# Eight mLSTM heads woven into projection products: 18 steps a head in place of 16, and the norm's products kept in VectorE's program order

## The chip, the cores and the metric

One Trainium2 chip, of which the kernel uses one core. The metric is the device time of one execution in microseconds (us). A core has a matrix engine (TensorE; PE in the profile, its weight loads PEld), VectorE (DVE), ScalarE (ACT), GpSimd (POOL) and SyncE (SP), each with its own in-order queue.

## The reference

The reference is one layer of a hybrid block over 256 latent and 256 context tokens of width 2048. It normalises and modulates the tokens, projects them with one wide matrix, and feeds two branches: a bidirectional mLSTM with eight heads (128 key and 256 value features each), and a bidirectional attention with 16 query heads. Both are gated, projected, merged by sigmoid gates, projected once more, and added to the stream with a layer norm. What the change touches is one mLSTM head of the latent tokens. Per head and direction it computes, with a state C that comes from the context tokens:

```
w = exp(d - m)                      decays between tokens, lower or upper triangle
s = (q k^T) * w
num = a * (C q) + s v
h = num / max(|den|, exp(-m))       both directions are summed
h = rms_norm(h) * mh_norm_w         then times sigmoid(o) * silu(z)
```

## The kernel before, in words

All arithmetic is in 32-bit floats. A product is made of three TensorE products of operands that are split into a high and a low part (`three`, L340 to L343, and `three_b`, L345 to L348); `split` (L335 to L338) makes the parts, the high one with a ScalarE cast (L337), the low one with a VectorE subtraction (L338). Weights come in 512 KB blocks (`raw`), are split the same way (`whi`, `wlo`) one block ahead of their use, and live in two or three buffers.

The large projections (`gemm_tok`, `gemm_feat`) run one after the other and keep TensorE fed. Everything else is cut into small tasks which `weave` spreads over a projection: a projection of 512 columns for two token tiles has 32 ticks (16 slices of the contraction, two token tiles), `tick` is called ahead of each, and with N tasks in the list, task i runs at the first tick that is not below 32 i / N. One tick's work is three TensorE products of 512 columns. A block of weights serves four ticks, and the next block's split is issued ahead of ticks 0, 4, 8 and so on. The instructions of one engine are then put in order by a list scheduler that models the engines' times: an instruction whose operands it takes to be there may be moved ahead of others that were written before it. Buffers are shared by tags, and an instruction waits for the release of its buffer.

A head (`head`, L831 to L941) is a generator, and each `yield` ends a step. The 16 steps before the change are, in order:

- 0: the rows of this head are fetched by a GpSimd DMA into `ws` (L842), the keys of the context are transposed (`pk`, L849), weighted on ScalarE (`kw`, L853), and split into `rd` together with the values
- 1: keys and queries are split into `rc`
- 2: empty
- 3 and 4: the state's products `pC` (six TensorE products each, out of `rd`), each split into `ra`
- 5: the decays `w`, in `ws`: four VectorE operations (L878 to L881), the exponential on ScalarE (L882), the product with q (L883), and a split into `rb`
- 6: the products q k (`pS`), and on VectorE `w` times them (L894, L897)
- 7: `w` is split (high part in `rb`, low part in `rc`: these are the rows `rb<-ws` on ScalarE and `rc<-ws` on VectorE), and the values are split into `ra`
- 8: empty
- 9 to 12: the four numerators `ph` (two token tiles, two directions), which need `ra`, `rb` and `rc`, and the division by the denominators
- 13: the reciprocal root of the mean square, `rr` (VectorE L128, then GpSimd L129)
- 14: the norm's products, two VectorE operations (L934) which multiply the head's output by `rr` and by the gate `G`
- 15: four transposes (`pT`, L940) and the split of their result for the next projection

The heads overlap. The last three steps of a head are inserted into the list of the next at positions 1, 7 and 10. A projection takes 16 tasks of the heads (`n = HEAD_STEPS`), so that the lists run like this: projection z of column block c carries head 2c from its step 2 on and begins head 2c+1 (steps 0 and 1); projection o of block c+1 does the same for head 2c+1. Two further tasks (`held`) are inserted at positions 1 and 4 of each list: in a z projection the sigmoid and norm weight of o (`put_o`), in an o projection the SiLU of z and its product into the gate `G` (`put_z`, four VectorE operations). So the gate that head 2c needs is completed in the next projection o, in the same list as that head's norm products; for head 2c+1 it is complete one list earlier. Head 7 runs in the projection q of the first attention group (`group`), with its own last steps and a few empty tasks behind it.

Only SyncE fetches the weights; the GpSimd queue carries the DMA of `ws`, the fetch of the norm's weights (`mh`), the powers `rr` and the product of o's sigmoid with the norm's weights.

Of the kernel before, what the change touches and what calls it, by code (L numbers as in the profile page):

```python
# [12 lines left out]
ALU = mybir.AluOpType  # L13
# [37 lines left out]
def block_kernel(ctx: ExitStack, tc: tile.TileContext, a: dict, out: bass.AP):  # L51
# [26 lines left out]
    def t2(n):  # L78
        return tp.tile([P, 512], F32, tag="T2", name=nm(n), bufs=4)


    def sm(n, w):
        return tp.tile([P, w], F32, tag=f"sm{w}", name=nm(n), bufs=SMALL[w])
# [20 lines left out]
    def halves(x):  # L104

        return x.rearrange("p (n w) -> p w n", w=2)

    def as_halves(x):
        return x.rearrange("p (w n) -> p w n", w=2)
# [225 lines left out]
    def split(hi, lo, src):  # L335

        nc.scalar.copy(hi, src)  # L337
        nc.vector.tensor_tensor(lo, src, hi.bitcast(F32), op=ALU.subtract)  # L338
# [39 lines left out]
    def steps(gen, n):  # L378

        return [lambda: next(gen, None) for _ in range(n)]  # L380
# [158 lines left out]
    end, j = 0.0, 0  # L539
    for i, (c, k0, k1) in enumerate(VISITS):  # L540
        end += (k1 - k0) * (1.8 if chunks[c][1] == "w_kv" else 2.65)
        j0, j = j, max(j, min(len(units), math.ceil((end - T0) * 6 / DT)))
# [127 lines left out]
    def conv(x, hd, n, scale):  # L670

        ac = t2("cva")[:, :n * 256].rearrange("p (s t) -> p s t", s=n)
        sg = t2("cvs")[:, :n * 256].rearrange("p (s t) -> p s t", s=n)
        nc.scalar.activation(ac, x[:, :, 1:257], AF.Identity, bias=cv[:, hd, 3:4], scale=cv[:, hd, 1:2])
        nc.vector.scalar_tensor_tensor(ac, x[:, :, 0:256], cv[:, hd, 0:1], ac, op0=ALU.mult, op1=ALU.add)
        nc.vector.scalar_tensor_tensor(ac, x[:, :, 2:258], cv[:, hd, 2:3], ac, op0=ALU.mult, op1=ALU.add)
        nc.scalar.activation(sg, ac, AF.Sigmoid)
        nc.vector.scalar_tensor_tensor(x[:, :, 1:257], ac, scale, sg, op0=ALU.mult, op1=ALU.mult)
# [75 lines left out]
    j = 32  # L754
# [35 lines left out]
    gate_of = [None] * 4  # L790
# [35 lines left out]
        held.extend(lambda t=t: put_z(t) for t in range(2))  # L826
        gate_of[c] = g_

    HEAD_STEPS = 16

    def head(h):  # L831
        c, j = h // 2, h % 2
# [3 lines left out]
        stt = nc.vector.scalar_tensor_tensor  # L836
# [23 lines left out]
        wl, kqh, kql = rc[:, 0:768], rc[:, 768:1280], rc[:, 1280:1792]  # L860
        split(kqh[:, 0:256], kql[:, 0:256], kl)
        split(as_halves(kqh[:, 256:512]), as_halves(kql[:, 256:512]), halves(q))
        yield
        yield

# [34 lines left out]
        split_v(vh, vl, va[c][:, 0:2, j, :])  # L900
        yield
        yield

        hh = t2("hh").rearrange("p (t d) -> p t d", t=2)
        intra = {(0, 0): [(0, 0)], (0, 1): [(128, 0), (640, 1)],
# [24 lines left out]
        rr = sm("rr", 2)  # L930
        rsqrt(rr, ss, 1.0 / 256.0, EPS)
        yield
        for t in range(2):
            stt(hh[:, t, :], hh[:, t, :], rr[:, t:t + 1], gate_of[c][:, t, j * 256:(j + 1) * 256],  # L934
                op0=ALU.mult, op1=ALU.mult)
        yield
        pT = aux("pT")
        for f in range(2):
# [29 lines left out]
    order = []  # L968
    for h in range(8):
        st = steps(head(h), HEAD_STEPS)  # L970
        if h > 0:
            for at, step in zip((1, 7, 10), order[-3:]):
                st.insert(at, step)
            order = order[:-3]
        order += st
    n = HEAD_STEPS
    order = [lambda h=h: conv(qT[:, h:h + 1, :], h, 1, 1.0) for h in range(8)] + order
# [294 lines left out]
```

## Time and profile before

| what | value |
|---|---|
| median of 3 runs | 1346.44 us (1344.09 to 1348.11) |
| the profiled execution's own time | 1343.62 us |
| its span, first to last instruction | 1341.6 us |
| mean granted TensorE clock | 0.991 |
| instructions | 19662 |

The span is that of the profiled execution; some 2 us of its time lie outside. In the rows further down, a timeline row gives start, duration, engine, line, operation, output and inputs, and in brackets how long the engine sat idle just before and what released it. A TensorE product's record is longer than the distance to the next product's start, since products are pipelined.

### The profile page before, as it was taken

What the parts mean: (1) busy time and instruction counts of PE and PEld (TensorE: products, weight loads), DVE (VectorE), ACT (ScalarE), POOL (GpSimd) and SP (SyncE); (2) the same over time, 40 slices, a digit from 0 to 9 for tenths busy, and PEclk for the clock granted to TensorE, in tenths of its full rate; (3) what the DMA queues carried; (4) which work ended last, traced back from release to release, by engine and by line L of the source; (5) the groups of instructions that cost most, each with busy time, mean ns of one, the idle gap of its engine ahead of it and who ended that gap; (6) DMA issues with size and microseconds to landing.
All of it is one profiled execution on the core that took longest, in us unless ns stands there. A gap on an engine that the chain in (4) does not pass through costs nothing.

```text
span 1341.6 us, 19662 instructions
## 1 busy us (share of the span) xinstructions
PE 1296.4 (97%) x7541; PEld 1161.7 (87%) x7541; DVE 976.0 (73%) x1577; ACT 649.8 (48%) x928; POOL 54.1 (4%) x83
## 2 busy tenths in 40 slices
PE   6999998999999999999999999999999999999996
PEld 3788988999999988888889999998888888888884
DVE  6698998877986678787787868786555455545667
ACT  4544322324334576676755566565444444434441
POOL 0000000000110011010110000000000000000000
PEclk8999998999999999999999999999999999999999
DMA  9876764885435554555455444445655556576663
GB/s 339 310 260 227 251 221 136 296 306 189 143 111 189 195 167 160 171 181 180 155 162 182 139 161 142 143 139 174 204 198 202 204 197 203 195 275 219 218 219 116
DMA packets 77902, 264.17 MB, mean 197 GB/s; under 512 B 8984, under 2 KB 11688, under 8 KB 77168
## 3 DMA queue, kind: packets, MB, share of 16 engines
q1 hardware_dynamic: 74752, 251.99, 55.5%
q0 software_dynamic: 2448, 10.68, 2.4%
q8 instruction: 59, 0.97, 0.3%
q10 hardware_dynamic: 608, 0.24, 0.1%
q14 instruction: 35, 0.29, 0.1%
HBM read 260.75 MB, written 2.14 MB: 196 GB/s over the span
## 4 chain that ended last, share of the span: by engine, by line
PE 46%; DVE 2%; ACT 1%; DMA 1%; issue 0%; DVEq 0%; ACTq 0%
PE zb L347 2%; PE zb L346 2%; PE zb L348 2%; PE yb L343 2%; PE yb L342 2%; PE yb L341 2%; PE ga L343 2%; PE ga L341 2%; PE ga L342 2%; PE ya L343 2%; PE ya L341 2%; PE ya L342 2%; PE gb L342 2%; PE gb L343 2%; PE gb L341 2%; PE q L342 2%
## 5 line engine op out<-in xcount | busy, mean ns | idle before, releaser
L338 DVE TENSOR_TENSOR wlo<-raw,whi 128x1024 fp32r<-128x1024 f32 (+3 forms) x375 | 445.3, 1190 | 264.5 <-ACT whi L337 259.4
L337 ACT CAST whi<-raw 128x1024 fp32r<-128x1024 f32 (+3 forms) x375 | 380.2, 1016 | 449.2 <-PE p L343 130.8
L342 PE MATMUL p<-wlo,u 128*128 128x512 f32 (+1 forms) x448 | 160.1, 357 | 2.5 <-DVE wlo L338 2.4
L341 PE MATMUL p<-whi,u 128*128 128x512 f32 (+1 forms) x448 | 159.3, 358 | 2.1 <-ACT u L302 1.1
L225 DVE SCALAR_TENSOR_TENSOR junk<-mod,sc 128x1024 bf16<-128x1024 f32 x128 | 153.4, 1221 | 9.4 <-DMA mod<-in_w_mod 9.3
L343 PE MATMUL p<-whi,u 128*128 128x512 f32 (+1 forms) x448 | 159.4, 356 | 0.0
L342 PEld LDWEIGHTS p<-wlo,u 128*128 128x128 f32 x448 | 86.5, 193 | 10.8 <-DVE wlo L338 4.2
L341 PEld LDWEIGHTS p<-whi,u 128*128 128x128 f32 x448 | 85.7, 192 | 11.5 <-ACT u L302 2.5
L343 PEld LDWEIGHTS p<-whi,u 128*128 128x128 f32 x448 | 86.6, 193 | 6.8
L346 PE MATMUL zb<-u,whi 128*128 128x256 f32 x256 | 72.0, 281 | 0.0
L346 PE MATMUL p<-u,whi 128*128 128x256 f32 x256 | 70.6, 278 | 0.7 <-ACT u L302 0.7
L348 PE MATMUL p<-u,wlo 128*128 128x256 f32 x256 | 70.3, 275 | 0.2 <-DVE wlo L338 0.2
L347 PE MATMUL zb<-u,whi 128*128 128x256 f32 x256 | 70.4, 275 | 0.0
L348 PE MATMUL zb<-u,wlo 128*128 128x256 f32 x256 | 70.4, 275 | 0.0
L347 PE MATMUL p<-u,whi 128*128 128x256 f32 x256 | 70.4, 275 | 0.0
L346 PEld LDWEIGHTS p<-u,whi 128*128 128x128 f32 x256 | 48.9, 192 | 2.1 <-ACT u L302 1.2
L341 PE MATMUL z<-whi,u 128*128 128x512 f32 x128 | 49.7, 389 | 0.0
L341 PE MATMUL q<-whi,u 128*128 128x512 f32 x128 | 49.7, 388 | 0.0
L347 PEld LDWEIGHTS p<-u,whi 128*128 128x128 f32 x256 | 49.1, 192 | 0.4 <-issue 0.4
L342 PE MATMUL gb<-wlo,u 128*128 128x512 f32 x128 | 48.7, 381 | 0.8 <-DVE wlo L338 0.8
L342 PE MATMUL z<-wlo,u 128*128 128x512 f32 x128 | 49.2, 384 | 0.2 <-DVE wlo L338 0.2
L348 PEld LDWEIGHTS p<-u,wlo 128*128 128x128 f32 x256 | 49.1, 192 | 0.3 <-DVE wlo L338 0.3
(329 smaller groups left out, 3156.9 us busy)
## 6 DMA issues: line engine op xcount, KB each, us to landing
mod<-in_w_mod SPq DMA_DIRECT2D x96, 512.0 KB, 4.9
raw<-in_w_g SPq DMA_DIRECT2D x64, 512.0 KB, 4.1
raw<-in_w_o SPq DMA_DIRECT2D x32, 512.0 KB, 3.5
raw<-in_w_z SPq DMA_DIRECT2D x32, 512.0 KB, 3.6
raw<-in_w_qb SPq DMA_DIRECT2D x32, 512.0 KB, 3.6
raw<-in_w_zb SPq DMA_DIRECT2D x32, 512.0 KB, 3.4
raw<-in_w_ba SPq DMA_DIRECT2D x32, 512.0 KB, 3.5
raw<-in_w_bb SPq DMA_DIRECT2D x32, 512.0 KB, 4.1
```

The lines of the kernel that those rows point to most:

```text
L225: nc.vector.scalar_tensor_tensor(junk, blk, 1.0, sc[v][:, hf * 1024:(hf + 1) * 1024], op0=ALU.mult, op1=ALU.mult, accum_out=mp[:, v, hf, j ...
L337: nc.scalar.copy(hi, src)
L338: nc.vector.tensor_tensor(lo, src, hi.bitcast(F32), op=ALU.subtract)
L341: mm(o, lhsT=xh, rhs=wh, start=start, stop=False)
L342: mm(o, lhsT=xh, rhs=wl, start=False, stop=False)
L343: mm(o, lhsT=xl, rhs=wh, start=False, stop=stop)
L346: mm(o, lhsT=wh, rhs=xh, start=start, stop=False)
L347: mm(o, lhsT=wh, rhs=xl, start=False, stop=False)
L348: mm(o, lhsT=wl, rhs=xh, start=False, stop=stop)
```

## The change

A head gets 18 steps. One empty step is added ahead of the state's products (there are two now), and one ahead of the numerators (two as well). The positions at which the last three steps of a head are inserted into the next head's list become 1, 8 and 12. The two products of the norm (L934) are pinned with `tc.keep_in_program_order`: the list scheduler may not put them ahead of any VectorE instruction that was written before them. This adds no semaphore wait. `HEAD_STEPS` also sets how many tasks of the list a projection takes (`n`), so that a projection still carries one head.

```diff
-    HEAD_STEPS = 16
+    HEAD_STEPS = 18
...
         split(as_halves(kqh[:, 256:512]), as_halves(kql[:, 256:512]), halves(q))
         yield
         yield
+        yield
...
         split_v(vh, vl, va[c][:, 0:2, j, :])
+        yield
         yield
         yield
...
         for t in range(2):
-            stt(hh[:, t, :], hh[:, t, :], rr[:, t:t + 1], gate_of[c][:, t, j * 256:(j + 1) * 256],
-                op0=ALU.mult, op1=ALU.mult)
+            tc.keep_in_program_order(
+                stt(hh[:, t, :], hh[:, t, :], rr[:, t:t + 1],
+                    gate_of[c][:, t, j * 256:(j + 1) * 256], op0=ALU.mult, op1=ALU.mult))
...
-            for at, step in zip((1, 7, 10), order[-3:]):
+            for at, step in zip((1, 8, 12), order[-3:]):
```

## Rows read from the trace of the kernel before

**Rows 1.** The page, busy time: engine, us (share of the span), instructions.

```profile
PE 1296.4 (97%) x7541; PEld 1161.7 (87%) x7541; DVE 976.0 (73%) x1577; ACT 649.8 (48%) x928; POOL 54.1 (4%) x83
```

**Rows 2.** Busy us by stretch: PE, PEld, DVE, ACT, POOL, PEclk, DMA share, GB/s.

```profile
463.00:700.00 237.00, 227.14 (x1239) 200.65 (x1238) 184.77 (x352) 160.57 (x264) 27.92 (x32) 0.99 0.51 168
526.00:530.00 4.00, 2.22 (x11) 1.49 (x10) 3.10 (x7) 3.98 (x8) 0.71 (x1) 0.99 0.11 45
530.00:533.40 3.40, 3.40 (x11) 2.89 (x12) 2.16 (x4) 3.39 (x7) 1.28 (x1) 0.51 0.44 154
```

**Rows 3.** Groups on PE, 440 to 700 us: busy, mean ns, idle before.

```profile
L343 PE MATMUL ph<-ra,rc 128*128 128x258 f32 x48 | 13.7, 286 | 3.1 <-DVE rc L338 3.0
L343 PE MATMUL pC<-rd 128*128 128x258 f32 x32 | 9.8, 308 | 5.7 <-DVE rd L338 5.6
```

**Rows 4.** Timeline of PE, head 4 in the third z projection.

```profile
586.36 0.28 PE L342 MATMUL pC<-rd 128*128 128x258 f32 x1
588.05 0.38 PE L343 MATMUL pC<-rd 128*128 128x258 f32 x1 [1.42 <-DVE rd L338]
...
588.48 0.28 PE L343 MATMUL pC<-rd 128*128 128x258 f32 x1
588.60 0.38 PE L341 MATMUL z<-whi,u 128*128 128x512 f32 x1
588.81 0.38 PE L342 MATMUL z<-wlo,u 128*128 128x512 f32 x1
...
601.29 0.28 PE L343 MATMUL ph<-ra,rc 128*128 128x258 f32 x1
```

**Rows 5.** Timeline of PE, the other heads' products that waited.

```profile
499.78 0.38 PE L343 MATMUL pC<-rd 128*128 128x258 f32 x1 [0.85 <-DVE rd L338]
...
513.95 0.38 PE L343 MATMUL ph<-ra,rc 128*128 128x258 f32 x1 [0.65 <-DVE rc L338]
...
528.26 0.38 PE L341 MATMUL pC<-rd 128*128 128x258 f32 x1 [0.67 <-ACT rd L337]
...
529.86 0.56 PE L343 MATMUL pC<-rd 128*128 128x258 f32 x1 [1.11 <-DVE rd L338]
...
572.66 0.38 PE L343 MATMUL ph<-ra,rc 128*128 128x258 f32 x1 [0.50 <-DVE rc L338]
...
644.75 0.38 PE L343 MATMUL pC<-rd 128*128 128x258 f32 x1 [1.35 <-DVE rd L338]
...
671.98 0.38 PE L343 MATMUL pC<-rd 128*128 128x258 f32 x1 [0.86 <-DVE rd L338]
...
685.22 0.38 PE L343 MATMUL ph<-ra,rc 128*128 128x258 f32 x1 [1.32 <-DVE rc L338]
```

**Rows 6.** Timeline of DVE ahead of head 4's state products.

```profile
585.37 0.88 DVE L934 SCALAR_TENSOR_TENSOR hh<-hh,rr,G 128x256 f32<-128x256 f32 x2 [0.90 <-POOL rr L129]
586.17 1.22 DVE L338 TENSOR_TENSOR wlo<-raw,whi 128x1024 fp32r<-128x1024 f32 x1
587.30 0.69 DVE L338 TENSOR_TENSOR rd<-kw,rd 128x512 fp32r<-128x512 f32 x1
```

**Rows 7.** Timeline of ACT ahead of head 4's state products.

```profile
578.60 1.28 ACT L882 ACT_TABLE_LOAD   x1 [3.23 <-DVE r L920]
...
584.51 1.06 ACT L337 CAST whi<-raw 128x1024 fp32r<-128x1024 f32 x1
```

**Rows 8.** Timeline of DVE, from head 4's score products to the next projection o.

```profile
595.26 2.35 DVE L338 TENSOR_TENSOR wlo<-raw,whi 128x1024 fp32r<-128x1024 f32 x2
597.53 0.68 DVE L894 TENSOR_TENSOR ws<-ws,pS 128x512 f32<-128x512 f32 x1
...
599.44 0.96 DVE L338 TENSOR_TENSOR rc<-ws,rb 128x768 fp32r<-128x768 f32 x1 [0.90 <-ACT rb L337]
...
604.49 0.48 DVE L878 SCALAR_TENSOR_TENSOR ws<-ws,gT,cst 128x256 f32<-128x256 f32 x1 [0.75 <-DMA ws<-rows]
...
622.32 0.88 DVE L934 SCALAR_TENSOR_TENSOR hh<-hh,rr,G 128x256 f32<-128x256 f32 x2
```

## The prediction

> **What bounds the kernel now.** I began with the page's busy times. PE is busy 97% of the span, no other engine over 87% [rows 1]: what delays no TensorE product costs nothing. Then the stretches: the heads run from 463 to 700 us, where PE is busy 227.1 of 237.0 us, so 9.9 us stand still by the busy column, while VectorE (78%) and ScalarE (68%) have room on average [rows 2]. Grouped by operation, nearly all of this idle time lies before two products: 5.7 us before the third product of a state triple, waiting for the low part of `rd`, and 3.1 us before a numerator, waiting for the low part of `rc` [rows 3].
>
> The timeline then prices one such wait. In head 4 the second state product starts at 586.36, the third at 588.05; with no wait they start 0.11 to 0.12 apart (588.48, 588.60). So 1.58 us are lost where the idle column says 1.42, because a record outlasts the distance to the next start [rows 4]. I add the same 0.17 to each idle time. The waits, head by head, are then [rows 5]: state products 1.02 (head 1), 0.84 and 1.28 (head 2), 1.58 (head 4), 1.52 (head 6), 1.03 (head 7); numerators 0.82 (head 1), 0.67 (head 3; head 5 has the same row), 1.49 (head 7). Even heads, which run in z projections, wait at the state, odd ones mostly at the numerators.
>
> A third loss follows from the second. From 526 to 530 us PE is busy only 2.22 of 4.00 us, and from 530.0 to 533.4 the granted clock is 0.51, the 1.2 GHz level [rows 2]: 0.49 x 3.4 = 1.67 us lost.
>
> By the Trainium skill ("Perfetto Trace Analysis", section "Identifying the Most-Contended Engine") a busy share of matmuls flatters, and the share of weight loads tells headroom better. That share is 200.65 of 237 us here [rows 2], and by it 36 us could be had. The distances between starts agree that the busy column says too little, but only by 0.17 us a wait; I go by them.
>
> **The change, part by part.** A tick is three products of 512 columns 0.215 us apart, 0.65 us [rows 4]. A list has 16 head tasks and 2 held ones over 32 ticks before, 18 and 2 after. Task i of N runs at the first tick from 32 i / N on, which gives, for heads 1 to 6 (before, after): first state product 4, 5; second 6, 8; decays 9, 10; norm's products 11, 12; score products 13, 13; split of `w` 15, 15; transposes 16, 18; numerators 20, 22, 24, 25 and 21, 23, 24, 26; next head's step 0 27, 28; root 29, 29; step 1 31, 31. Nothing is removed or added but order, so no engine's busy time changes.
>
> *Numerators.* They come one tick later behind the split, 6 instead of 5. What they wait for is VectorE's `rc`, whose chain starts at the score products, and those stay at tick 13. Heads 1, 3 and 5 gain one tick each of their 0.82, 0.67, 0.67: 1.95 us. Head 7's list has 22 tasks before and 24 after (its own last steps and four empty tasks are in it); the split is at tick 12 in both, the numerators go from 16 to 18: two ticks, 1.29 of its 1.49. Sum 3.24.
>
> *State products.* Step 0 moves from 27 to 28, so from `pk` to the first state product it is 9 ticks as before, and if the wait were counted from `pk`, the new step would bring nothing. It isn't: ScalarE runs without a pause from the table load at 578.60 to the cast of 584.51, just ahead of `rd` [rows 7], and that load waited 3.23 us for VectorE's decays, which themselves wait for the DMA of `ws` [rows 8]. This DMA goes out when the previous head's split of `w` frees its buffer. So step 0's later tick costs nothing (its DMA on GpSimd's queue is released by the buffer, its transposes are long done when `kw` starts), and the clock of this wait runs from the previous head's split. Where the numerators before it waited too (ahead of heads 2, 4, 6), the tick has been counted there already: zero. Where they didn't (heads 1 and 7) the products come 0.65 later against the chain: 1.30.
>
> *The pin, where it helps.* For odd heads the gate is complete when `rr` is, and the scheduler puts L934 at the front, ahead of the next head's weight split and `rd`. VectorE idles 0.90 us for GpSimd's `rr` and works 0.88 on it [rows 6]. Gone, these are not 1.78 us: the `wlo` behind it needs the cast that ends at 584.51 + 1.06 = 585.57 [rows 7], and starts at 586.17 [rows 6]. So `rd` comes 0.60 earlier, three times (heads 2, 4, 6): 1.80. Bounds 0 and 3 x 1.58. What is late next is ScalarE's cast.
>
> *The pin, where it costs.* The pair now stands where it is written, behind the `wlo` of tick 12 and ahead of L894 in the z projections. VectorE has no gap there: two `wlo` splits stand directly before L894, which starts without idle time [rows 8]. Behind it wait L897, ScalarE's high split, `rc`, the numerators, the next `ws` fetch. In head 4 `rc` ends at 599.44 + 0.96 = 600.40 [rows 8] and the numerator that needs it runs at 601.29 [rows 4], 1.54 us of room with the added tick, so 0.88 doesn't reach the numerators; it reaches the next head's decays, through the `ws` fetch. Between 0 (the second `wlo` falls behind L894, or a VectorE pause takes the pair) and 0.88, three times; I take the middle, as each row is equally near: 1.32. For even heads the pair stands at 622.32, in the projection where it is written [rows 8]: zero.
>
> *The rest.* The transposes come two ticks later, and with them the cast and subtraction of `pT`; still three ticks before the numerators. That the second held task now stands before the second state product moves one sigmoid by one tick: zero, ScalarE has pauses such as the 3.23 us [rows 7]; without that cover, some tenths of a us.
>
> *The clock.* Head 2's two waits, 2.12 us together, shrink by 0.60. The other waits of 1.5 us left the clock up, so the low stretch may go. Half of 1.67: 0.83; bounds 0 and 1.67. By the Trainium skill ("TensorE: Matmul & The Clock Gate", "Part 1: The HAM clock gate") the gate goes by how busy PE has just been. The one low stretch behind the stretch at 2.22 of 4.00 agrees, and by that rule the whole 1.67 would more likely come back.
>
> **Sum.** 3.24 + 1.30 + 1.80 - 1.32 + 0.83 = 5.85 us. Against the profiled execution's 1343.62 us that is 1337.8. It lies 2.8 us under the median of the runs shown, so against the median: 1346.4 - 5.8 = 1340.6.
>
> **Rivals.** *The chain is the period.* If the chain through VectorE and ScalarE from one split of `w` to the next, rather than TensorE, sets a head's time, a later product only moves the wait. Then only head 7's 1.29 and head 1's 0.65 are had: 1344.5, no measurable change. For it: VectorE stands without idle time before L894 and L934 [rows 8]. Against: both engines have idle time in every projection [rows 2, 7], and that chain holds ticks of TensorE too, which the step shortens.
>
> *The norm in front of the scores.* The pinned pair could go behind one `wlo` while L894 still falls behind the other: 0.88 + 1.22 = 2.10 us later in three z projections, less the tick 1.45 at the odd heads' state products, 4.35; in three o projections 1.22 - 0.65 = 0.57, 1.71; one more stretch at the low clock, 1.67; less the pin's 1.80 and head 1's 0.65: 5.3 us slower, 1351.7. It decides once L894 in a z projection starts over 1.5 us later against the score products than before. For it: the gap-free queue [rows 8]; against: the scheduler may put L894 before the second `wlo`.
>
> *All waits go.* 5.7 + 3.1 us [rows 3], nine times 0.17, and 1.67: 12.0 us, 1334.4. It needs a shorter chain, for which only the pin stands.
>
> *It doesn't do what it says.* A step added among the same 32 ticks is a tick only by rounding; the scheduler may order TensorE's products otherwise. That would give the first rival's time or less, and is counted with it.
>
> **How the numbers follow.** The forecast has 0.52, the chain as period 0.31, all waits gone 0.06, the norm in front 0.11. A measurement of this kernel can tell about 0.3% from no change, 4.0 us: faster means under 1342.4, slower over 1350.5. The forecast's unknowns (pin help 0 to 4.7, pin cost 0 to 2.6, clock 0 to 1.7) carry it from 1336 to 1343, a small part of it above 1342.4: faster 0.56, same 0.33, slower 0.11. The range, 1335.5 to 1347.5, leaves out the norm in front and all waits gone, 0.17 together; the forecast's own range is 1336 to 1343.
>
> **What would show it.** Right: the idle time before `ph<-rc` falls from 3.1 to under 1 us, that before `pC<-rd` from 5.7 to about 3; no L934 waits for `rr` at a z projection's start; the granted clock near 530 us is 1.0. Wrong: `pC` waits as long as before (first rival), L894 late with odd heads' `pC` waits grown (second), or new idle time before the projections' own products on `wlo`.

## The result and the profile after

The change makes the kernel slower: a median of 1361.51 us (1359.19 to 1364.94, four runs) against 1345.26 us for the kernel before (1342.61 to 1348.11, four runs), a ratio on record of 1.0138 with a 95% interval of 1.0113 to 1.0163 (the two medians alone give 1.0121). The forecast was 1340.6, and its range ended at 1347.5. The profiled execution of the changed kernel took 1359.19 us, its span 1357.4 us at a mean granted clock of 0.988 (before 0.991).

No engine got more work. The page's busy times, which answer to [rows 1], grow by 4.9 us on PE and by less than 1 us anywhere else:

```profile
PE 1301.3 (96%) x7541; PEld 1161.9 (86%) x7541; DVE 973.3 (72%) x1577; ACT 650.1 (48%) x928; POOL 54.7 (4%) x83
```

Where the time went is found by comparing the stretch from the first product of the first o projection to the first product that follows the heads (`zb`), the same work in both kernels. First before, then after, with the columns of [rows 2]:

```profile
448.20:698.90 250.70, 240.84 (x1298) 212.55 (x1297) 195.07 (x366) 169.76 (x279) 27.92 (x32) 0.99 0.51 169
```

```profile
444.70:714.60 269.90, 249.43 (x1298) 216.93 (x1297) 193.58 (x366) 170.37 (x279) 28.23 (x32) 0.96 0.47 158
```

It grew by 269.90 - 250.70 = 19.2 us, with the same 1298 products. (The run had come to it 3.5 us earlier, so the whole run lost less. The opening stretch, which the change doesn't touch, ends anywhere between 444.7 and 453.6 us in the profiles of the runs below; so it is the heads' stretch that is compared here, from one profile of each kernel.) Of the 19.2, PE's idle time is 20.47 - 9.86 = 10.6 us, and its busy time grew by 8.6 us because the granted clock fell from 0.99 to 0.96: a share of 0.04 of 269.9 us is 10.8 us lost, before 0.01 of 250.7 was 2.5, and the difference is 8.3. Two losses, then: waits of TensorE, and low clock behind them. The groups on PE in that stretch, which answer to [rows 3], say which waits:

```profile
L341 PE MATMUL z<-whi,u 128*128 128x512 f32 x128 | 51.8, 405 | 1.6 <-ACT whi L337 1.6
L342 PE MATMUL z<-wlo,u 128*128 128x512 f32 x128 | 51.1, 399 | 2.3 <-DVE wlo L338 2.3
...
L343 PE MATMUL ph<-ra,rc 128*128 128x258 f32 x48 | 13.2, 275 | 0.0
...
L343 PE MATMUL pC<-rd 128*128 128x258 f32 x32 | 10.9, 341 | 3.6 <-DVE rd L338 3.4
L341 PE MATMUL pC<-rd 128*128 128x258 f32 x32 | 10.7, 334 | 12.2 <-ACT rd L337 12.2
```

The numerators' 3.1 us are gone, as intended, and the third state products wait 3.6 in place of 5.7. But the first state products of heads 1 to 7 now wait 12.2 us together, and they wait for ScalarE's cast, the high part of `rd`. Before, their row was:

```profile
L341 PE MATMUL pC<-rd 128*128 128x258 f32 x32 | 9.2, 288 | 0.7 <-ACT rd L337 0.7
```

Here is head 4 on PE after the change:

```profile
592.75 0.38 PE L341 MATMUL pC<-rd 128*128 128x258 f32 x1 [2.03 <-ACT rd L337]
...
594.14 0.58 PE L343 MATMUL pC<-rd 128*128 128x258 f32 x1 [0.90 <-DVE rd L338]
```

The cast itself is as short as ever. What is new is the order on ScalarE in front of it (in both kernels L853 computes `kw` and L812 is o's sigmoid; L929 of the changed kernel is the sum of squares `sq`). Before, only the cast of weights of [rows 7] stood between `kw` and its cast, and the sigmoid's table load came behind:

```profile
583.51 1.12 ACT L853 ACTIVATE kw<-pk,gT 128x128 f32<-128x128 f32 x4
...
585.44 0.64 ACT L337 CAST rd<-kw 128x512 fp32r<-128x512 f32 x1
...
586.77 1.28 ACT L812 ACT_TABLE_LOAD   x1
```

After:

```profile
588.74 0.42 ACT L929 ACTIVATE sq<-hh 128x256 f32<-128x256 f32 x1 [1.04 <-DVE hh L927]
...
589.15 1.12 ACT L853 ACTIVATE kw<-pk,gT 128x128 f32<-128x128 f32 x4
590.29 1.28 ACT L812 ACT_TABLE_LOAD   x1
591.59 0.60 ACT L812 ACTIVATE G<-o 128x512 f32<-128x512 f32 x1
592.08 0.61 ACT L337 CAST rd<-kw 128x512 fp32r<-128x512 f32 x1
```

Two things are late. Between `kw` (done at 590.27) and its cast, ScalarE loads a table and runs a sigmoid, 1.28 + 0.60 us; and `kw` itself starts only after ScalarE has idled 1.04 us for VectorE's `hh`, the result of the previous head's last numerator. These two are the whole delay: from the table load of the decays' exponential to the cast of `kw`, ScalarE took 585.44 - 578.60 = 6.84 us before and takes 592.08 - 582.29 = 9.79 now, 2.95 more, and 1.04 + 1.28 + 0.60 is 2.92 (the cast of weights has only changed its place, from behind `kw` to ahead of it). VectorE shows why `hh` is late. First before (L920, L921 and L925 are there what L922, L923 and L927 are in the changed kernel), then after:

```profile
580.40 0.16 DVE L920 TENSOR_TENSOR r<-ph,r 128x1 f32<-128x1 f32 x1
580.59 0.16 DVE L921 RECIPROCAL r<-r 128x1 f32<-128x1 f32 x1
581.53 0.48 DVE L925 SCALAR_TENSOR_TENSOR hh<-ph,r,hh 128x256 f32<-128x256 f32 x1 [0.78 <-ACT hh L923]
582.46 1.23 DVE L338 TENSOR_TENSOR wlo<-raw,whi 128x1024 fp32r<-128x1024 f32 x1 [0.45 <-ACT whi L337]
```

```profile
584.23 0.14 DVE L921 SCALAR_TENSOR_TENSOR r<-ph,gT 128x1 f32<-128x1 f32 x1
586.15 1.23 DVE L338 TENSOR_TENSOR wlo<-raw,whi 128x1024 fp32r<-128x1024 f32 x1 [1.77 <-ACT whi L337]
587.29 0.15 DVE L922 TENSOR_TENSOR r<-ph,r 128x1 f32<-128x1 f32 x1
...
588.03 0.15 DVE L923 RECIPROCAL r<-r 128x1 f32<-128x1 f32 x1
588.22 0.48 DVE L927 SCALAR_TENSOR_TENSOR hh<-ph,r,hh 128x256 f32<-128x256 f32 x1
```

L921, L922 and L923 are the division of the last numerator. Before, they stood together, and `hh` followed ahead of the weight subtraction. Now a weight subtraction `wlo` stands between the first and the second: it waits 1.77 us for its cast and works 1.23, and behind it wait the rest of the division, `hh`, `sq`, `kw`, and at last `rd`. The same row stands within the last division ahead of heads 2, 3, 5, 6 and 7 too (waits of 1.78, 1.56, 1.48, 1.78 and 1.51 us). Ahead of head 1 it does not; there only a table load and a sigmoid have come between `kw` and its cast, and the first state product waits 1.89 us. The list scheduler has put VectorE and ScalarE in another order; that is the change's effect that the prediction left out.

The clock falls behind such waits. In head 4, TensorE works 0.97 of the 3.90 us from 590.7, and for the next 5.4 us it is granted 0.50, the 1.2 GHz level:

```profile
590.70:594.60 3.90, 0.97 (x5) 0.76 (x5) 1.88 (x3) 3.89 (x7) 1.36 (x2) 0.81 0.37 134
594.60:600.00 5.40, 5.40 (x18) 4.58 (x18) 3.60 (x5) 2.82 (x5) 2.17 (x1) 0.50 0.38 131
```

Behind the waits of heads 1, 2 and 6 it is granted 0.50 for a while as well; behind those of heads 3, 5 and 7, where the longest is 1.72 us, it stays at 1.00.

### The profile page after: what moved, and what is told of

Same layout as the page of the kernel before. It is cut to its first block, busy times and chain, and to the rows that moved or that the text cites. A ratio compares the mean times of both kernels' runs of the same rounds, so it can differ in the third digit from the quotient of the medians.

```text
span 1357.4 us, 19655 instructions
## 1 busy us (share of the span) xinstructions
PE 1301.3 (96%) x7541; PEld 1161.9 (86%) x7541; DVE 973.3 (72%) x1577; ACT 650.1 (48%) x928; POOL 54.7 (4%) x83
## 4 chain that ended last, share of the span: by engine, by line
PE 78%; DVE 9%; issue 4%; DMA 4%; ACT 4%; POOL 1%; SPq 0%; DVEq 0%; ACTq 0%; POOLq 0%
PE p L342 5%; PE p L343 5%; PE p L341 5%; PE p L346 2%; DVE junk L225 2%; PE zb L348 2%; PE zb L347 2%; PE zb L346 2%; DVE wlo L338 2%; PE p L347 2%; PE p L348 2%; PE yb L342 2%; PE yb L343 2%; PE yb L341 2%; PE q L342 2%
## 5 line engine op out<-in xcount | busy, mean ns | idle before, releaser
L341 PE MATMUL p<-whi,u 128*128 128x512 f32 (+1 forms) x448 | 157.9, 355 | 2.6 <-ACT whi L337 1.4
L343 PE MATMUL p<-whi,u 128*128 128x512 f32 (+1 forms) x448 | 157.1, 351 | 0.0
L341 PEld LDWEIGHTS p<-whi,u 128*128 128x128 f32 x448 | 84.6, 189 | 12.5 <-ACT u L302 2.5
L342 PEld LDWEIGHTS p<-wlo,u 128*128 128x128 f32 x448 | 84.9, 189 | 10.8 <-DVE wlo L338 4.2
L343 PEld LDWEIGHTS p<-whi,u 128*128 128x128 f32 x448 | 84.8, 189 | 6.8
L341 PE MATMUL z<-whi,u 128*128 128x512 f32 x128 | 51.8, 405 | 1.6 <-ACT whi L337 1.6
L343 PE MATMUL z<-whi,u 128*128 128x512 f32 x128 | 50.6, 395 | 0.0
L341 PE MATMUL q<-whi,u 128*128 128x512 f32 x128 | 49.7, 388 | 0.0
L341 PE MATMUL o<-whi,u 128*128 128x512 f32 x128 | 49.4, 386 | 0.0
```

What stands on the lines that cost most here:

```text
L341: mm(o, lhsT=xh, rhs=wh, start=start, stop=False)
L342: mm(o, lhsT=xh, rhs=wl, start=False, stop=False)
L343: mm(o, lhsT=xl, rhs=wh, start=False, stop=stop)
```

## The experiments

Several of the expectations name theories by letters: A, that the moved steps do it, B that the pin does it, D that the buffer of `ws` ties the heads together. Ratios are to the kernel before on the same chip, with the 95% interval.

**Which half of the change?** Two runs, each with one half: `pin_only` has the pinned L934 and 16 steps, `steps_only` 18 steps and no pin.

> 16 steps as before, only the norm's products (L934) pinned. Theory A (step 0 fell behind the weight split of tick 28, and ScalarE's sigmoid with its table load now stands between kw and rd): the pin is no part of the loss, the time is that of the kernel before or up to 3 us under it (0.997 to 1.001), and the state products wait about 5 us in all or less. Theory B (the pinned products hold up VectorE): most of the 16 us loss is here, 1.007 or more.

> 18 steps as in the changed kernel, the norm's products not pinned. Theory A: the whole loss stays, 1.010 to 1.016 of before, with about 12 us of idle time before the state products on ScalarE's rd, and three stretches at the low clock. Theory B: the loss is gone, 0.995 to 1.002.

`pin_only`: 1345.18 us, 1.0012 [0.9994, 1.0030]. `steps_only`: 1361.3 us, 1.0134 [1.0107, 1.0160], with 12.5 us of idle time before the first state products. The steps carry the whole loss, and the pin is neither the harm nor a gain: with it alone the third state products wait as long as before, and the numerators and first state products a little longer (3.8 us in place of 3.1, 1.6 in place of 0.7).

```profile
L343 PE MATMUL ph<-ra,rc 128*128 128x258 f32 x48 | 13.9, 290 | 3.8 <-DVE rc L338 3.7
...
L343 PE MATMUL pC<-rd 128*128 128x258 f32 x32 | 9.5, 297 | 5.7 <-DVE rd L338 5.7
```

**Which tick?** With the lists of o and z spread over 31 ticks, the next head's step 0 is back at tick 27 and the last numerator at 25; the added steps and the pin stay.

```diff
-        weave(spread_in(tasks[0]), 32)
+        weave(spread_in(tasks[0]), 31)
...
-        weave(spread_in(tasks[1]), 32)
+        weave(spread_in(tasks[1]), 31)
```

> The changed kernel, its lists in the o and z projections spread over 31 ticks instead of 32: step 0 goes back from tick 28 to 27, ahead of the weight split of tick 28; numerators at 21, 22, 24, 25, state products at 5 and 8, the pin stays. Theory A: the cast of weights stands between kw and rd again, no table load, and the time falls by 13 to 20 us to 0.994 to 1.001 of before. Theory B, and a theory C (later products fill the lists and push the splits together): no more than 3 us of the loss comes back, 1.010 or more.

1344.28 us, 1.0007 [0.9990, 1.0024]: the loss is gone. The waits that the change aimed at are small, and others have come up in their place, at the projections' own products:

```profile
L342 PE MATMUL o<-wlo,u 128*128 128x512 f32 x128 | 49.4, 386 | 3.6 <-DVE wlo L338 3.6
L342 PE MATMUL z<-wlo,u 128*128 128x512 f32 x128 | 49.4, 386 | 2.9 <-DVE wlo L338 2.5
...
L343 PE MATMUL ph<-ra,rc 128*128 128x258 f32 x48 | 13.9, 290 | 1.2 <-DVE rc L338 1.1
...
L343 PE MATMUL pC<-rd 128*128 128x258 f32 x32 | 8.9, 278 | 0.8 <-DVE rd L338 0.8
```

Without the pin (`ticks31_nopin`, the same lists):

> 18 steps over 31 ticks, norm's products not pinned: tells what the pin is worth once step 0 is in its old place. The prediction's terms say 1.8 us for the pin less 1.3 against it: within 1 us of the 31-tick kernel with the pin (1344.3 us, 1.0007). If the pin gave back more, this one is 3 us or more slower.

1343.33 us, 0.9987 [0.9972, 1.0003]: no difference that can be told from the run with it.

**Is it the sigmoid on ScalarE?** In the changed kernel, the sigmoids of o and z are queued behind the cast of `kw`.

```diff
-        split(kwh, kwl, kw)
+        cast[:] = [nc.scalar.copy(kwh, kw)]
+        nc.vector.tensor_tensor(kwl, kw, kwh.bitcast(F32), op=ALU.subtract)
...
+        with tc.issue_after(cast[0].ins):
+            nc.scalar.activation(dst, src, AF.Sigmoid)
```

> The changed kernel, with the sigmoids of o and z queued on ScalarE behind the cast kw to rd of the head (issue order alone). Step 0 stays at tick 28. Theory A: with the table load out of the way (1.28 + 0.60 us) most of the wait of the state products goes, and 10 us or more of the 16 come back: 0.997 to 1.004 of before. If the weight cast ahead of kw is the larger part, half or less comes back: 1.007 or more. Theory B: nothing comes back.

1356.86 us, 1.0098 [1.0068, 1.0128]. The loss falls from 1.38 to 0.98% (the two intervals overlap a little), and the mean granted clock rises from 0.988 to 0.993, but most of it stays. The first state products wait 2.5 us in place of 12.2; now it is the projections' products that wait, whose `whi` and `wlo` come late:

```profile
L341 PE MATMUL z<-whi,u 128*128 128x512 f32 x128 | 49.6, 387 | 2.5 <-ACT whi L337 2.5
...
L342 PE MATMUL z<-wlo,u 128*128 128x512 f32 x128 | 49.1, 384 | 4.6 <-DVE wlo L338 4.6
L342 PE MATMUL o<-wlo,u 128*128 128x512 f32 x128 | 49.1, 384 | 4.4 <-DVE wlo L338 4.4
...
L341 PE MATMUL pC<-rd 128*128 128x258 f32 x32 | 9.5, 297 | 2.5 <-ACT rd L862 2.4
```

So the sigmoid is a part of it and not the root. The weight subtraction still stands within the last division there, in head 4 with this wait:

```profile
590.62 1.22 DVE L338 TENSOR_TENSOR wlo<-raw,whi 128x1024 fp32r<-128x1024 f32 x1 [1.78 <-ACT whi L337]
```

**Do the empty steps matter at all?** `step0_late` is the kernel before, with no empty step and no pin, and its lists spread over 32.5 ticks. That moves step 0 from 27 to 28, the last numerator from 25 to 26, the transposes from 16 to 17 and the decays from 9 to 10.

> The kernel before, its lists in the o and z projections spread over 32.5 ticks instead of 32: of the 16 steps' ticks, step 0 goes from 27 to 28 (behind that tick's weight split), the last numerator from 25 to 26, the transposes from 16 to 17, the decays from 9 to 10; no empty step, no pin. Theory A (step 0 against the weight split is the cause): the loss appears here too, 1.007 to 1.014 of before, with the sigmoid's table load between kw and rd and the state products waiting over 8 us in all. Theory C (the two empty steps are the cause): as before, 0.998 to 1.003.

1363.23 us, 1.0135 [1.0111, 1.0158], with 11.8 us before the first state products: the whole loss without the steps. I took step 0 for the cause then, and tested it alone against the last numerator alone, both in the kernel before. A step with `at` is held until that tick:

```diff
+            if pace[0] < getattr(todo[0], "at", 0):
+                break
...
+            st[0].at = 28
```

(heads 1 to 7, `step0_only`), or, in `numer_only`, `st[12].at = 26` for heads 0 to 6.

> The kernel before, with nothing but step 0 of heads 1 to 7 held back from tick 27 to 28. On ScalarE the weight cast now stands ahead of kw, but no table load between kw and rd. Theory A (step 0 against the weight split): 1.008 to 1.014 of before. Theory A2 (the last numerator's move from 25 to 26 is what lets the sigmoid in): 0.998 to 1.005.

> The kernel before, with nothing but the last numerator of heads 0 to 6 held back from tick 25 to 26; step 0 stays at 27. The sigmoid with its table load stands between kw and rd for heads 2 to 7. Theory A: 0.998 to 1.003. Theory A2: nearly all of the loss, 1.008 to 1.014, state products waiting over 8 us in all.

`step0_only`: 1349.22 us, 1.0036 [1.0019, 1.0054]. `numer_only`: 1359.36 us, 1.0125 [1.0087, 1.0164]. My theory named the wrong one of the two moved steps. The last numerator's tick makes nearly the whole loss; step 0's makes a small one of its own, and elsewhere. First `step0_only`, then `numer_only`:

```profile
L341 PE MATMUL z<-whi,u 128*128 128x512 f32 x128 | 50.8, 397 | 5.9 <-ACT whi L337 5.9
...
L341 PE MATMUL pC<-rd 128*128 128x258 f32 x32 | 9.0, 281 | 0.6 <-ACT rd L337 0.5
```

```profile
L341 PE MATMUL pC<-rd 128*128 128x258 f32 x32 | 11.4, 355 | 13.9 <-ACT rd L337 13.9
```

And `numer_only` has both marks of the changed kernel: on VectorE a `wlo` that waits for its cast, ahead of the last division, and on ScalarE the table load between `kw` and its cast.

```profile
587.56 1.22 DVE L338 TENSOR_TENSOR wlo<-raw,whi 128x1024 fp32r<-128x1024 f32 x1 [2.16 <-ACT whi L337]
```

```profile
590.76 1.12 ACT L855 ACTIVATE kw<-pk,gT 128x128 f32<-128x128 f32 x4
591.90 1.28 ACT L814 ACT_TABLE_LOAD   x1
593.19 0.60 ACT L814 ACTIVATE G<-o 128x512 f32<-128x512 f32 x1
593.69 0.61 ACT L337 CAST rd<-kw 128x512 fp32r<-128x512 f32 x1
```

**Is the order the cause?** Now the changed kernel with its ticks as they are, and the orders mended. `both_after` queues the sigmoids as above and keeps the weights' subtractions of the o and z projections in the order in which they are written; `subs_kept` does the second alone (`keep` is set while the o and z projections are written):

```diff
-            split(hi, lo, raw)
+            nc.scalar.copy(hi, raw)
+            sub_ = nc.vector.tensor_tensor(lo, raw, hi.bitcast(F32), op=ALU.subtract)
+            if keep:
+                tc.keep_in_program_order(sub_)
```

> The changed kernel with the sigmoids queued behind the cast kw to rd, and in addition the weights' subtractions of the o and z projections kept in the order they are written in on VectorE, so that none stands between the parts of the last numerator's division. If these two orders are the whole loss: 0.998 to 1.004 of before. If the second is no part of it: as with the first alone, 1.007 to 1.013. A subtraction kept in order may also come late for its own projection, which would show as waits on wlo: over 1.013.

> The changed kernel with one thing more: the weights' subtractions of the o and z projections kept in written order on VectorE; the sigmoids are free. In the schedule this alone takes the sigmoid and its table load out from between kw and rd. If the weight subtraction inside the last numerator's division is the root: 0.998 to 1.003 of before, as with both orders kept (1.0002). If the sigmoid's own order is a loss apart: 1.003 or more.

`both_after`: 1344.68 us, 1.0002 [0.9986, 1.0019]. `subs_kept`: 1346.29 us, 1.0003 [0.9985, 1.0022]. Keeping one kind of VectorE instruction in its place takes the whole loss away, with the last numerator at tick 26 and step 0 at 28. (What keeping them does in the kernel before was not run.) In `subs_kept`, `hh` (here L939) runs ahead of the subtraction, and that one no longer waits:

```profile
584.18 0.48 DVE L939 SCALAR_TENSOR_TENSOR hh<-ph,r,hh 128x256 f32<-128x256 f32 x1 [0.27 <-ACT hh L937]
584.59 1.22 DVE L329 TENSOR_TENSOR wlo<-raw,whi 128x1024 fp32r<-128x1024 f32 x1
```

ScalarE's order then mends itself: the cast of `kw` follows `kw`, and the table load comes 0.8 us behind it.

```profile
586.16 1.14 ACT L864 ACTIVATE kw<-pk,gT 128x128 f32<-128x128 f32 x4
587.33 0.62 ACT L866 CAST rd<-kw 128x512 fp32r<-128x512 f32 x1
...
588.73 1.28 ACT L800 ACT_TABLE_LOAD   x1
```

No state product waits any more, and the numerators 1.0 us in place of 3.1. Yet nothing is gained, since the waits have gone to the projections' products:

```profile
L345 PE MATMUL o<-wlo,u 128*128 128x512 f32 x128 | 49.2, 385 | 5.9 <-DVE wlo L329 5.8
L345 PE MATMUL z<-wlo,u 128*128 128x512 f32 x128 | 49.2, 385 | 5.8 <-DVE wlo L329 5.8
...
L346 PE MATMUL ph<-ra,rc 128*128 128x258 f32 x48 | 13.4, 279 | 1.0 <-DVE rc L341 1.0
...
L346 PE MATMUL pC<-rd 128*128 128x258 f32 x32 | 8.9, 278 | 0.0
```

**Another way at the chain.** The prediction saw the heads tied together by the buffer of `ws`. `ws_own_buffer` is the kernel before with that tile from the other set of buffers:

```diff
-        ws = wslot("ws")
+        ws = slot("ws")
```

> The kernel before, with the tile ws taken from the other set of large buffers, so that the fetch of the next head's rows no longer waits for the split of w of this head. Theory D (the chain from one head's split of w through the fetch, the decays and the exponential to the next state products sets a head's time): waits of state products and numerators fall and the kernel is 4 to 12 us faster, 0.991 to 0.997. Theory E (the order on ScalarE and VectorE alone sets it, the fetch is hidden): no change, 0.999 to 1.002.

1340.56 us, 0.9965 [0.9951, 0.9980]: faster. The mechanism that was expected is not shown, though: the state products wait 3.2 us (third) and 2.6 us (first), the numerators 2.8, 8.6 us together against 9.5 before, and the stretch of the heads took 249.3 us against 250.7 in single profiles. Why it is faster stays open. With the added steps it was tried three ways: over 31 ticks with the pin (`ticks31_ws_own`), without it (`steps31_ws_own`), and in the changed kernel with both orders kept (`kept_ws_own`).

> The 31-tick kernel (18 steps, pin) with ws in the other set of buffers. Theory D: faster than before by more than the 16-step kernel with that buffer, since later products now meet a shorter chain: 0.988 to 0.995. Theory E: as the 31-tick kernel, 0.999 to 1.002.

> 18 steps over 31 ticks, norm's products not pinned, ws in the other set of buffers: the parts that did not lose. If they add up (0.9987 and 0.9965): 0.993 to 0.997 of before. If the waits only move to the projections' own weights, as in the 31-tick kernel: 0.997 to 1.001.

> The changed kernel with both orders kept and ws in the other set of buffers, a candidate to beat both kernels. If the order and the buffer add up: 0.993 to 0.997 of before. If the waits move to the projections' weights once more: 0.997 to 1.001.

They took 1342.18 us, 0.9982 [0.9964, 1.0001]; 1341.17 us, 0.9978 [0.9957, 0.9999]; and 1338.76 us, 0.9964 [0.9949, 0.9979]. The last beats both kernels (the kernel before took 1344.04 beside it), but by no more than the buffer alone does without the steps. In its single profile the heads' stretch took 244.6 us, 4.7 less than with the buffer alone; the run times don't show that.

## Why the prediction was wrong

- The step that failed is what the sum made of the sentence that closes the list of ticks, "Nothing is removed or added but order, so no engine's busy time changes". It is true of busy time ([rows 1] and the page after), but the new order on VectorE and ScalarE was priced only around the norm's products. The later last numerator was counted for its own wait alone, and what may slip in front of the work behind it was put at nothing. The runs showed that this one tick costs 1.25% (`numer_only`, 1.0125 [1.0087, 1.0164]), where its term had a gain. *It doesn't do what it says* raised a new order too, but for TensorE's products alone.
- *Numerators* (3.24 us gained). The wait did go, from 3.1 to 0.0, so what the step said of `rc` was right. It left out what leans on the last numerator from behind: its division, `hh`, `sq`, and through ScalarE's queue the next head's `kw` and `rd`. One tick later, a weight subtraction gets in between; `numer_only` prices that at 1.25% of 1344.18, 16.8 us (its medians lie 15.2 apart), and `subs_kept` takes it away.
- *The rest* (zero, "some tenths of a us" without cover). It weighed the second of the two sigmoids, a tick earlier, against ScalarE's pauses. What came between `kw` and its cast is the first one, whose tick (2) didn't move, with a table load of 1.28 us. With the sigmoids queued behind the cast (`sigmoid_after`), 0.40% comes back, some 5 us.
- *State products* (1.30 gained, step 0 for nothing). They wait 15.8 us in place of 6.4 (L341 and L343 together). "So step 0's later tick costs nothing" was wrong too, if by less: 0.36%, 4.8 us, in `step0_only`, at the z projections' own `whi`. Only the step's DMA, transposes and the start of `kw` had been weighed, not what it may delay; which of its instructions does so was not tried.
- *The pin* (1.80 gained, 1.32 paid). Neither end can be told from the times: `pin_only` 1.0012 [0.9994, 1.0030], and 1.0007 against 0.9987 with and without it over 31 ticks. The gain's mechanism isn't seen either: in `pin_only` the third state products wait 5.7 us, as before.
- *The clock* (0.83 gained). With no `pC` wait left it does come back: in `subs_kept` the granted clock of the heads' stretch is 1.00, before 0.99 [rows 2]. In the changed kernel it went the other way, some 8 us lost, with four low stretches in place of one. By the Trainium skill ("TensorE: Matmul & The Clock Gate", "Part 1: The HAM clock gate") the gate goes by how busy PE has just been; the 5.4 us at 0.50 behind 0.97 busy of 3.90 agree.
- *The norm in front of the scores* gave 5.3 us more than before, a third of the loss, by another mechanism, and was not what happened: L894 (L895 in the changed kernel) starts 1.2 us behind the last score product in each of the three z projections, no later than before, the numerators behind it don't wait at all, and without the pin (`steps_only`) the loss is the same.
- *The chain is the period* (1344.5) has the time that the change gives once the order is mended: `ticks31`, `both_after` and `subs_kept` lie within 0.1% of before. Its sign, `pC` waiting as long as before, did not come; the waits turned up at `wlo`, which the prediction had listed as a sign of its own. So the waits did move, but that the chain from one split of `w` to the next is what moved them is not shown. In none of these three kernels did the forecast's gain come.
- Most signs of being right came true in a kernel that is 1.4% slower: the idle time before `ph<-rc` fell to 0.0, that before the third state products to 3.6, and no L934 (L937 in the changed kernel) waits for `rr` at a z projection's start. They watched the products that the change aimed at, and the loss came at the first state products. Only the clock near 530 us was not as the signs had it: 0.50 from 532 to 534.

What made the scheduler put the subtraction there is not measured. What is seen is that with the last numerator at tick 25 it stands behind the last division ahead of heads 3 to 7 (ahead of heads 1 and 2 one stands within the last division but one, and starts without idle time), and in the changed kernel within the last one ahead of heads 2 to 7, waiting. Why the table load gets in between `kw` and its cast ahead of head 1 is open; in `subs_kept` that is gone too.

## What to carry to other kernels

Where a list scheduler orders the engines, a step moved by one tick can change the queues of engines that it hardly uses: compare every engine's order, and ask what may now slip into a dependent chain, above all an instruction that itself waits. Here it was enough to keep that instruction in its place, with every step at its new tick. And when a wait of TensorE is taken away, look for where it comes back: here as many us turned up at the next products that need VectorE. Last, signs that watch only the waits that a change aims at can all come true while the kernel gets slower; sum the idle time before every group of products.

## What the runs showed of the hardware

The sum of TensorE's idle time alone doesn't tell the granted clock. In `sigmoid_after`, TensorE stands still for 237.00 - 217.56 = 19.4 us in the heads' stretch, about as long as in the changed kernel (20.5 us in its longer stretch), but in waits of at most 1.02 us, and the granted clock stays at 1.00:

```profile
463.00:700.00 237.00, 217.56 (x1160) 186.08 (x1159) 172.56 (x326) 153.22 (x253) 23.57 (x25) 1.00 0.47 158
```

In the changed kernel, with waits of 2.03 and 0.90 us at head 4's state products, it falls to 0.50 for 5.4 us; it falls behind head 1's single wait of 1.89 us too. ScalarE's table load took 1.28 us each time it stood in the chain, twice the cast that waited behind it.
